# Moving the two halves of half of the weights by 64 and by 192 bytes inside their buffers

## The chip, the cores and the metric

The kernel runs on one core of a Trainium2 chip. The metric is the time of one execution on the device in microseconds (us). The kernel before takes 2594.1 us (median of three runs, 2593.63 to 2594.11).

## What is computed

The reference is a decoder trunk of two layers over 256 tokens with 2048 features, all in float32. Cut to what matters here, a layer is a row of large matrix products with small pieces of attention between them:

```python
proj = rms_norm(x, mix_norm) @ w_in              # 2048 x 6924
...
x = x + mix @ w_out                              # 2048 x 2048
x = x + cross_attention(rms_norm(x, xattn_norm), rms_norm(mem, mem_norm), wq, wk, wv, wo)
u = rms_norm(x, ffn_norm) @ ffn_w_up             # 2048 x 11264
...
x = x + (silu(gate) * val) @ ffn_w_down          # 5632 x 2048
```

The four head groups between `w_in` and `w_out` (retention, stick-breaking attention, HGRN2, sparse attention) and the cross-attention are small beside these products.

## The kernel before

**Products in three parts.** TensorE (PE in the profile) multiplies in the type float32r, which keeps fewer bits than float32. So the kernel splits each operand into a high part `hi` (the value rounded to float32r) and a low part `lo` (what is left), and adds three products: hi·hi, lo·hi and hi·lo. The activations are split when they are made, into tiles `xt` and `mg` of 128 x 2 x 256 elements: for 128 features the high parts of 256 tokens and then their low parts, 2048 bytes in each partition.

**Units of weights.** The weights come from memory in units of at most 128 x 1024 elements, 4096 bytes in each partition, in the order that `plan()` fixes. SyncE (SP) issues the transfer of a unit into a buffer `raw` (`u_dma`) six units ahead of its use. ScalarE (ACT) rounds it into `hi` (`u_hi`, L409) three units ahead, and VectorE (DVE) writes `lo` = raw - hi (`u_lo`, L415, which the profile shows at the helper's line L250) two units ahead. There are five buffers `raw`, four `hi` and three `lo`.

**Two kinds of use.** A matmul on PE has an operand that is loaded into the array first (`lhsT`, 128 columns; the profile's engine PEld shows the load) and one that is streamed through it (`rhs`, up to 512 columns). The load for the next matmul runs beside the stream of the present one.

- By feature (`group_b`): the weights are loaded and the activations are streamed. A unit gives 8 matmuls of 512 columns at L493, each with a slice of 128 columns (512 bytes) of `hi` loaded and a whole `xt` tile streamed, and then 8 matmuls of 256 columns at L496, with slices of `lo` loaded and the high half of the same `xt` tiles streamed. 448 units are used in this way, those of `ffn_w_up` among them.
- By token (`group_a`, and `group_tail` for the last of them): the activations are loaded and the weights are streamed. A unit of 1024 elements gives 12 matmuls of 512 columns at L424, L425 and L426. Some units are narrower: 396 and 384 columns for parts of `w_in`, 256 columns for the values of the cross-attention.

**Where the buffers lie.** The pool `flow` lays out `raw`, `hi`, `lo`, `xt` and `mg` one behind the other in SBUF. A first tile of 1920 bytes, named `edge` (L208), brings the first `raw` to a multiple of 2048 bytes. Buffers of 4096 and 2048 bytes follow, so each of these tiles begins at a multiple of 2048 bytes, and each slice that is loaded or streamed begins at a multiple of 512 bytes. The one exception is the second half of a unit of 396 columns, whose stream begins 1584 bytes behind the start of its buffer.

**Order of the work.** The program is written in the order of the units (the last loop of `body`): for each unit the transfer six ahead, the `hi` three ahead, the `lo` two ahead, the unit's matmuls, and a step (`tick`) of the smaller work, which lives in generators. No scheduler reorders it.

Of the kernel before, what the change touches and what calls it, by code (L numbers as in the profile page):

```python
# [9 lines left out]
F32 = mybir.dt.float32  # L10
F32R = mybir.dt.float32r
# [122 lines left out]
def shape_consts():  # L134
    f = np.float32
    i = np.arange(128)
    c = {}
    lg = np.log1p(-np.exp2(-5.0 - np.arange(H)))
    rel = (i[None, :] - i[:, None]).astype(np.float64)
    dec = np.zeros((128, H, 2, 128))  # L140
    for h in range(H):
        dec[:, h, 0] = np.where(rel >= 0, np.exp(lg[h] * np.maximum(rel, 0)), 0.0)
        dec[:, h, 1] = np.exp(lg[h] * (rel + 128))
    ident = np.eye(128)
    ones = np.ones((128, 128))
    tri = (i[:, None] >= i[None, :]) * 1.0
    M = np.zeros((128, 5, 128), np.float32)
    for n in range(128):
        M[n // 8 * 8:n + 1, 0, n] = 1
        for e, b in enumerate((8, 16, 32, 64)):  # L150
            mid = n // (2 * b) * 2 * b + b
            if n >= mid:
                M[mid - b:mid, 1 + e, n] = 1
    sbm = np.where(i[:, None] < i[None, :], 0.0, NEG)
    cm = np.concatenate([np.zeros((128, 128)), np.where(i[None, :] > i[:, None], NEG, 0.0)], axis=1)
    last = np.arange(15) * 16 + 31
    ok = np.stack([last[None, :] <= (t * 128 + i)[:, None] for t in range(2)], axis=1)
    inv = (10000.0 ** (-(np.arange(64) / 64))).astype(f)
    half_pi = np.full((128, 1), np.pi / 2)
    parts = [("ident", ident), ("ones", ones), ("inv", np.broadcast_to(inv, (128, 64))), ("hpi", half_pi),  # L160
             ("eps", np.full((128, 1), EPS)),
             ("tri", tri), ("dec", dec * SCALE), ("sbm", sbm), ("cm", cm),
             ("sel", (i[:, None] % 32 == np.arange(15)[None, :]) * 1.0), ("cadd", np.where(ok, 0.0, NEG)), ("cmul", ok * 1.0)]
    off, cols = {}, 0
    for n, a in parts:
        w = a.reshape(128, -1).shape[1]
        off[n] = (cols, w)
        cols += w
    big = np.concatenate([a.reshape(128, -1).astype(f) for _, a in parts], axis=1)
    return off, np.ascontiguousarray(big), M  # L170
# [18 lines left out]


class Unit:
    __slots__ = ("off", "cols", "nk", "pe", "end", "ks", "raw", "hi", "lo", "at")


def body(ctx, tc, w, x, xt_in, mem, mem_t, pos, consts, masks, pars, wck, wcv, fnorm, out):
    nc = tc.nc
    AHEAD, HI, LO = 6, 3, 2
    off, _, _ = shape_consts()
# [3 lines left out]
    flow = ctx.enter_context(tc.tile_pool(name="flow", bufs=1))  # L202
# [7 lines left out]
    def nm(p):  # L210
        count[0] += 1
        return f"{p}{count[0]}"
# [10 lines left out]
    def acc(shape):  # L223
        return pp.tile(shape, F32, name=nm("acc"), tag="acc", bufs=4)
# [4 lines left out]
    def f(ap):  # L229
        return ap.bitcast(F32)  # L230
# [18 lines left out]
    def tt(o, a, b, op):  # L249
        V.tensor_tensor(o, a, b, op=op)  # L250
# [102 lines left out]
    def start(gen):  # L353
        front.append(gen)
# [25 lines left out]

    units = []

    def unit(pe, end, ks):
        u = Unit()
        spec = next(units_w)
        u.off, u.nk = cursor[0], len(spec[2])
        u.cols = sum(b - a for a, b in spec[3])
        u.pe, u.end, u.ks = pe, end, ks
        u.raw = u.hi = u.lo = None
        cursor[0] += 128 * u.nk * u.cols  # L390
        units.append(u)

    def parts_of(u):

        n = u.nk * u.cols
        return ((0, n // 2), (n // 2, n)) if u.off == 0 else ((0, n),)
# [7 lines left out]

    def u_hi(u):
        n = u.nk * u.cols
        u.hi = flow.tile([128, n], F32R, name=nm("hi"), tag="hi", bufs=HI + 1, padded_shape=[128, 1024])
        for a, b in parts_of(u):
            A.copy(u.hi[:, a:b], u.raw[:, a:b])  # L409

    def u_lo(u):
        n = u.nk * u.cols
        u.lo = flow.tile([128, n], F32R, name=nm("lo"), tag="lo", bufs=LO + 1, padded_shape=[128, 1024])
        for a, b in parts_of(u):
            tt(u.lo[:, a:b], u.raw[:, a:b], f(u.hi[:, a:b]), OP.subtract)  # L415
        u.raw = None
# [11 lines left out]
    def group_a(src, klists, n, end, st=None, first=True, last=True):  # L428

        st = {} if st is None else st  # L430
        z = len(klists) - 1
        for i, kl in enumerate(klists):
            def pe(u, i=i, kl=kl):
                if first and i == 0:
                    st["ps"] = [acc([128, 512]) for _ in range(2)]
                for j, k in enumerate(kl):
                    mm_a(u, st["ps"], src(k), j, n, first and i == 0 and j == 0,
                         last and i == z and j == len(kl) - 1)

            def done():  # L440
                start(end(st.pop("ps")))
            unit(pe, done if last and i == z else None, lambda kl=kl: tuple(src(k) for k in kl))
        return st

    def group_tail(src, klists, n, end):
# [18 lines left out]
        for i, kl in enumerate(klists):  # L464
            def pe(u, i=i, kl=kl):
                if i == 0:
                    st["ps"] = [acc([128, 512]), acc([128, 512]), wk([128, 512])]
                if i < z - LO:
                    for p in range(3):
                        products(u.hi, u.lo, kl, i, p)  # L470
                elif i == z - LO:
                    late.extend((units[u.at + d].hi, units[u.at + d].lo, klists[i + d], i + d) for d in range(LO + 1))
                    for p in range(3):
                        for v in late:
                            products(*v, p)
                        end(p, st["ps"][p])
                    del late[:]
            unit(pe, None,
                 lambda i=i: tuple(src(k) for kl in (klists if i >= z - LO else klists[:i + 1]) for k in kl))
            units[-1].at = len(units) - 1  # L480

    def group_b(src, ends, order):


        sts = [{} for _ in ends]
        for g, i in order:
            def pe(u, i=i, st=sts[g]):
                if i == 0:
                    st["ps"] = [acc([128, 2, 256]) for _ in range(2)]
                xk = [src(4 * i + kk) for kk in range(4)]  # L490
                tiles = [(kk, q, kk * 256 + q * 128) for kk in range(4) for q in range(2)]
                for kk, q, at in tiles:
                    T.matmul(st["ps"][q].rearrange("p a b -> p (a b)"), lhsT=u.hi[:, at:at + 128],  # L493
                             rhs=xk[kk].rearrange("p a b -> p (a b)"), start=i == 0 and kk == 0, stop=False)
                for kk, q, at in tiles:
                    T.matmul(st["ps"][q][:, 1, :], lhsT=u.lo[:, at:at + 128], rhs=xk[kk][:, 0, :], start=False,  # L496
                             stop=i == 3 and kk == 3)

            def done(st=sts[g], end=ends[g]):
                start(end(st.pop("ps")))  # L500
            unit(pe, done if i == 3 else None, lambda i=i: tuple(src(4 * i + kk) for kk in range(4)))

    def whole(ps):

# [156 lines left out]
    def layer(l):  # L661
# [579 lines left out]
        for g, kind, segs in IN_GROUPS:  # L1241
            n = sum(SEG[s][1] - SEG[s][0] for s in segs)
            if kind == "A":
                group_a(src, pairs(range(8)), n, evs[g])
            else:
                group_b(src, [evs[g]] * 2, PAIR if g == "gq" else APART)
# [144 lines left out]

        at1 = len(units)
        group_b(lambda k: nx.k[k], [ev_xq] * 2, PAIR)
        group_b(lambda k: nm_.k[k], [ev_xk] * 2, APART)
        for v in range(2):
            group_a(lambda k: nm_.k[k], [range(4 * j, 4 * j + 4) for j in range(4)], 256, ev_xv(v))
# [163 lines left out]
    n = len(units)  # L1560
# [10 lines left out]
    first = first_norm()  # L1571
    first_parts = parts_of(units[0])
    u = units[0]
    u.hi = flow.tile([128, 1024], F32R, name=nm("hi"), tag="hi", bufs=HI + 1)
    u.lo = flow.tile([128, 1024], F32R, name=nm("lo"), tag="lo", bufs=LO + 1)
    tiles = xT.pop(0)
    for h, (a, b) in enumerate(first_parts):
        xk = [xt_tile("xt") for _ in range(2)]
# [6 lines left out]
        tt(u.lo[:, a:b], u.raw[:, a:b], f(u.hi[:, a:b]), OP.subtract)  # L1585
    u.raw = None
    u_hi(units[1])
    u_lo(units[1])
    next(first)
    u_hi(units[2])  # L1590
    next(first)
    start(first)
    for i in range(n):
# [8 lines left out]
        u = units[i]  # L1602
# [77 lines left out]
```

## Time and profile before

| | |
|---|---|
| median of three runs | 2594.1 us |
| the profiled execution: its own time | 2593.32 us |
| its span, first to last instruction | 2591.5 us |
| granted TensorE clock | 0.999 of full speed |
| PE busy | 2573.8 us, 99% of the span |
| DVE busy | 1778.5 us, 69% |
| ACT busy | 1364.5 us, 53% |

PE is busy throughout. A matmul's record in the profile is longer than the distance to the next one, because matmuls overlap; so what a matmul costs is read as the distance from its start to the start of the next, and not as its duration. The timeline merges neighbouring matmuls of one line into one row with their count, and gives starts to 0.01 us. Over a run of many matmuls the distance of one comes out to a fraction of a nanosecond.

### The profile page before, as it was taken

The numbers are of one execution on the slowest core, as the hardware profiler recorded it, in microseconds if no ns is written. First come the engines' busy times: TensorE is split into PE (matmuls) and PEld (weight loads), VectorE is DVE, ScalarE is ACT, GpSimd is POOL, SyncE is SP. The second block draws the span as 40 slices with busy tenths as digits, with TensorE's granted clock in tenths as the row PEclk, the third lists the DMA queues.
The fourth block names the chain that finished last, engine by engine and source line by source line (L and its number), as shares of the span: only waits on it lengthen the run. The fifth ranks groups of instructions, "written<-read, shape, count | busy, mean of one in ns | idle before, by whom it ended". The sixth has DMA issues, their size and how long they took to land. (4 is left out here: it accounts for less than half of the span.)

```text
span 2591.5 us, 37308 instructions
## 1 busy us (share of the span) xinstructions
PE 2573.8 (99%) x13866; PEld 2215.8 (86%) x13866; DVE 1778.5 (69%) x2881; ACT 1364.5 (53%) x2158; POOL 45.1 (2%) x79
## 2 busy tenths in 40 slices
PE   9999999999999999999999999999999999999998
PEld 7888888988888888888889888889888888888887
DVE  7776665667767676676768666656676666766766
ACT  6545545566455555454555455455654545454554
POOL 0010000000000000000000100000000000000000
PEclk9999999999999999999999999999999999999999
DMA  8574466545555555555555644655455565555664
GB/s 284 173 234 140 147 206 217 183 153 188 191 187 193 190 191 188 194 184 192 186 183 160 227 134 155 203 184 178 156 187 195 188 193 187 195 187 189 209 189 146
DMA packets 136582, 483.66 MB, mean 187 GB/s; under 512 B 15952, under 2 KB 16464, under 8 KB 136400
## 3 DMA queue, kind: packets, MB, share of 16 engines
q1 hardware_dynamic: 131024, 464.75, 54.7%
q0 software_dynamic: 4800, 15.73, 1.9%
q8 instruction: 109, 1.79, 0.3%
q10 hardware_dynamic: 576, 0.79, 0.1%
q14 instruction: 73, 0.60, 0.1%
HBM read 479.12 MB, written 2.10 MB: 186 GB/s over the span
## 5 line engine op out<-in xcount | busy, mean ns | idle before, releaser
L250 DVE TENSOR_TENSOR lo<-raw,hi 128x1024 fp32r<-128x1024 f32 (+3 forms) x881 | 1067.3, 1213 | 742.8 <-issue 264.1
L409 ACT CAST hi<-raw 128x1024 fp32r<-128x1024 f32 (+2 forms) x879 | 917.1, 1044 | 1151.0 <-PE acc L493 501.1
L493 PE MATMUL acc<-xt,hi 128*128 128x512 f32 x3456 | 870.5, 394 | 5.7 <-ACT hi L1584 5.7
L493 PEld LDWEIGHTS acc<-xt,hi 128*128 128x128 f32 x3456 | 623.7, 189 | 121.6 <-ACT hi L1584 5.7
L496 PEld LDWEIGHTS acc<-xt,lo 128*128 128x128 f32 x3456 | 472.3, 191 | 33.9
L496 PE MATMUL acc<-xt,lo 128*128 128x256 f32 x3456 | 482.6, 283 | 0.0
L424 PE MATMUL acc<-hi,mg 128*128 128x512 f32 (+1 forms) x1136 | 433.1, 381 | 0.2
L426 PE MATMUL acc<-hi,mg 128*128 128x512 f32 (+1 forms) x1136 | 428.8, 377 | 0.0
L425 PE MATMUL acc<-lo,mg 128*128 128x512 f32 (+1 forms) x1136 | 428.7, 377 | 0.0
L424 PE MATMUL acc<-hi,xt 128*128 128x512 f32 (+2 forms) x640 | 252.1, 394 | 0.0
L426 PEld LDWEIGHTS acc<-hi,mg 128*128 128x128 f32 x1136 | 213.7, 188 | 39.8 <-DVE mg L250 0.3
L424 PEld LDWEIGHTS acc<-hi,mg 128*128 128x128 f32 x1136 | 213.8, 188 | 39.3 <-ACT mg L263 1.0
L425 PEld LDWEIGHTS acc<-lo,mg 128*128 128x128 f32 x1136 | 213.9, 188 | 38.4
L426 PE MATMUL acc<-hi,xt 128*128 128x512 f32 (+2 forms) x640 | 243.2, 380 | 0.0
L425 PE MATMUL acc<-lo,xt 128*128 128x512 f32 (+2 forms) x640 | 242.8, 379 | 0.0
L253 DVE SCALAR_TENSOR_TENSOR s<-s,par,s 128x255 f32<-128x255 f32 x352 | 161.8, 480 | 6.3
L425 PEld LDWEIGHTS acc<-lo,xt 128*128 128x128 f32 x640 | 120.4, 188 | 20.8 <-issue 1.9
L424 PEld LDWEIGHTS acc<-hi,xt 128*128 128x128 f32 x640 | 120.3, 188 | 20.8 <-issue 2.3
L426 PEld LDWEIGHTS acc<-hi,xt 128*128 128x128 f32 x640 | 120.1, 188 | 20.6
L245 ACT ACTIVATE s<-s,par 128x256 f32<-128x256 f32 x176 | 96.1, 594 | 0.4 <-DVE s L250 0.4
L250 DVE TENSOR_TENSOR s<-acc,s 128x256 f32<-128x256 f32 x224 | 83.8, 416 | 0.0
L250 DVE TENSOR_TENSOR x<-x,acc 128x512 f32<-128x512 f32 x128 | 81.6, 678 | 1.5 <-PE acc L462 1.5
(202 smaller groups left out, 1421.9 us busy)
## 6 DMA issues: line engine op xcount, KB each, us to landing
raw<-in_w_dram SPq DMA_DIRECT2D x847, 512.0 KB, 3.4
raw<-in_w_dram SPq DMA_DIRECT2D x16, 396.0 KB, 3.1
raw<-in_w_dram SPq DMA_DIRECT2D x16, 384.0 KB, 3.1
s<-in_nsa_w_ck_dram POOLq DMA_DIRECT2D x16, 256.0 KB, 5.4
s<-in_nsa_w_cv_dram POOLq DMA_DIRECT2D x16, 256.0 KB, 4.8
s<-in_memt_dram POOLq DMA_DIRECT2D x16, 256.0 KB, 5.3
s<-in_xt_dram SPq DMA_DIRECT2D x8, 256.0 KB, 6.5
x<-in_x_dram SPq DMA_DIRECT2D x8, 256.0 KB, 7.1
```

What stands on the lines that cost most here:

```text
L245: A.activation(o, i, func, bias=bias, scale=scale)
L250: V.tensor_tensor(o, a, b, op=op)
L253: V.scalar_tensor_tensor(o, a, s, b, op0=op0, op1=op1)
L409: A.copy(u.hi[:, a:b], u.raw[:, a:b])
L424: T.matmul(ps[t][:, 0:n], lhsT=xh, rhs=hi, start=first, stop=False)
L425: T.matmul(ps[t][:, 0:n], lhsT=xh, rhs=lo, start=False, stop=False)
L426: T.matmul(ps[t][:, 0:n], lhsT=xl, rhs=hi, start=False, stop=last)
L493: T.matmul(st["ps"][q].rearrange("p a b -> p (a b)"), lhsT=u.hi[:, at:at + 128], rhs=xk[kk].rearrange("p a b -> p (a b)"), start=i == 0 an ...
L496: T.matmul(st["ps"][q][:, 1, :], lhsT=u.lo[:, at:at + 128], rhs=xk[kk][:, 0, :], start=False, stop=i == 3 and kk == 3)
```

## The change

The helper `unit` takes a flag `by_feature`, which `group_b` sets. The buffers `hi` and `lo` become 1088 elements (4352 bytes) instead of 1024 (4096 bytes). In a by-feature unit the low part begins 16 elements (64 bytes) behind the start of its buffer, and the high part 48 elements (192 bytes). In a by-token unit both begin at the start.

4352 is 2048 x 2 + 256. So neighbouring buffers of one kind stand 256 bytes further on, taken modulo 2048: the four `hi` buffers begin at 0, 256, 512 and 768 past a multiple of 2048, the three `lo` buffers at 0, 256 and 512. Two more filling tiles, `edge1` (1024 bytes, behind `hi`) and `edge2` (1280 bytes, behind `lo`), bring what follows back to multiples of 2048. All other tiles stand where they stood modulo 2048; they begin 4096 bytes later. By-feature slices of `hi` so begin at 192 past a multiple of 256, those of `lo` at 64 past a multiple of 256; by-token slices begin at multiples of 256.

On every engine the built program has the same instructions in the same order with the same waits. Only addresses differ.

```diff
+    def lo_tile(u):
+
+        o = flow.tile([128, 1088], F32R, name=nm("lo"), tag="lo", bufs=LO + 1)
+        at = 16 if u.by_feature else 0
+        return o[:, at:at + u.nk * u.cols]
+
+    def hi_tile(u):
+
+        o = flow.tile([128, 1088], F32R, name=nm("hi"), tag="hi", bufs=HI + 1)
+        at = 48 if u.by_feature else 0
+        return o[:, at:at + u.nk * u.cols]
...
     def u_hi(u):
         n = u.nk * u.cols
-        u.hi = flow.tile([128, n], F32R, name=nm("hi"), tag="hi", bufs=HI + 1, padded_shape=[128, 1024])
+        u.hi = hi_tile(u)
...
     def u_lo(u):
         n = u.nk * u.cols
-        u.lo = flow.tile([128, n], F32R, name=nm("lo"), tag="lo", bufs=LO + 1, padded_shape=[128, 1024])
+        u.lo = lo_tile(u)
...
-            unit(pe, done if i == 3 else None, lambda i=i: tuple(src(4 * i + kk) for kk in range(4)))
+            unit(pe, done if i == 3 else None, lambda i=i: tuple(src(4 * i + kk) for kk in range(4)), True)
...
-    u.hi = flow.tile([128, 1024], F32R, name=nm("hi"), tag="hi", bufs=HI + 1)
-    u.lo = flow.tile([128, 1024], F32R, name=nm("lo"), tag="lo", bufs=LO + 1)
+    u.hi = hi_tile(u)
+    flow.tile([128, 256], F32, name="edge1", tag="edge1")
+    u.lo = lo_tile(u)
+    flow.tile([128, 320], F32, name="edge2", tag="edge2")
```

## Rows read from the trace of the kernel before

**Rows 1.** The page's first and second part: busy time, share of the span and count of instructions of each engine, and the granted clock in 40 equal slices of the span (9 is 90% or more).

```profile
span 2591.5 us, 37308 instructions
PE 2573.8 (99%) x13866; PEld 2215.8 (86%) x13866; DVE 1778.5 (69%) x2881; ACT 1364.5 (53%) x2158; POOL 45.1 (2%) x79
PEclk9999999999999999999999999999999999999999
```

**Rows 2.** The waits of PE over the whole span: engine, tile and line that waited, whom it waited for, us in total, times, longest.

```profile
PE acc L493 <- ACT hi L1584: 5.7, 1, 5.7
PE wk L1381 <- ACT s L1370: 1.3, 2, 0.7
PE wk L1101 <- DVE s L250: 1.0, 2, 0.5
...
PE acc L461 <- DVE lo L250: 0.2, 1, 0.2
```

**Rows 3.** The groups of matmuls by line and shape: count, busy us, mean ns of one, idle before. The first two and the last are by feature, the others by token.

```profile
L493 PE MATMUL acc<-xt,hi 128*128 128x512 f32 x3456 | 870.5, 394 | 5.7 <-ACT hi L1584 5.7
L496 PE MATMUL acc<-xt,lo 128*128 128x256 f32 x3456 | 482.6, 283 | 0.0
L424 PE MATMUL acc<-hi,mg 128*128 128x512 f32 x1008 | 395.3, 392 | 0.2
...
L424 PE MATMUL acc<-hi,xt 128*128 128x512 f32 x512 | 207.6, 405 | 0.0
...
L493 PE MATMUL acc<-mg,hi 128*128 128x512 f32 x128 | 32.0, 392 | 0.0
```

**Rows 4.** The timeline of PE where by-token units (L424 to L426) give way to 32 by-feature units of `ffn_w_up` and come back: start us, us to the end of the row's last matmul, line, shape, count. Left out are 29 pairs of rows of the same kind.

```profile
850.35 0.39 PE L426 MATMUL acc<-hi,mg 128*128 128x512 f32 x1
850.58 1.98 PE L493 MATMUL acc<-xt,hi 128*128 128x512 f32 x8
852.39 1.12 PE L496 MATMUL acc<-xt,lo 128*128 128x256 f32 x8
853.35 2.00 PE L493 MATMUL acc<-xt,hi 128*128 128x512 f32 x8
855.19 1.11 PE L496 MATMUL acc<-xt,lo 128*128 128x256 f32 x8
856.14 2.00 PE L493 MATMUL acc<-xt,hi 128*128 128x512 f32 x8
...
937.14 2.00 PE L493 MATMUL acc<-xt,hi 128*128 128x512 f32 x8
938.99 1.11 PE L496 MATMUL acc<-xt,lo 128*128 128x256 f32 x8
939.94 0.40 PE L424 MATMUL acc<-hi,mg 128*128 128x512 f32 x1
```

**Rows 5.** The timeline of PE inside by-token work of 512 columns, first and last of 19 rows in a line.

```profile
276.63 0.39 PE L426 MATMUL acc<-hi,xt 128*128 128x512 f32 x1
...
280.71 0.39 PE L426 MATMUL acc<-hi,xt 128*128 128x512 f32 x1
```

**Rows 6.** The same inside by-token work of 256 columns, first and last of 27 rows in a line.

```profile
505.27 0.28 PE L426 MATMUL acc<-hi,mg 128*128 128x256 f32 x1
...
508.39 0.28 PE L425 MATMUL acc<-lo,mg 128*128 128x256 f32 x1
```

**Rows 7.** The timeline of PE after a piece of small matmuls (L1184), where by-token work of 512 columns begins again. Eleven rows in a line stand from 364.64 to 366.95.

```profile
364.33 0.48 PE L424 MATMUL acc<-hi,mg 128*128 128x512 f32 x1
364.64 0.40 PE L425 MATMUL acc<-lo,mg 128*128 128x512 f32 x1
...
366.26 0.40 PE L426 MATMUL acc<-hi,mg 128*128 128x512 f32 x1
366.50 0.39 PE L424 MATMUL acc<-hi,mg 128*128 128x512 f32 x1
...
366.95 0.39 PE L426 MATMUL acc<-hi,mg 128*128 128x512 f32 x1
```

**Rows 8.** The timeline of PE in by-token units of 396 columns: the last matmul of one unit (101.37), then a unit's six with its first half (101.55 to 102.45, streamed from the start of the buffer) and its six with the second half (102.63 to 103.53, streamed from 1584 bytes behind it).

```profile
101.37 0.34 PE L426 MATMUL acc<-hi,xt 128*128 128x396 f32 x1
101.55 0.34 PE L424 MATMUL acc<-hi,xt 128*128 128x396 f32 x1
...
102.45 0.34 PE L426 MATMUL acc<-hi,xt 128*128 128x396 f32 x1
102.63 0.34 PE L424 MATMUL acc<-hi,xt 128*128 128x396 f32 x1
...
103.53 0.34 PE L426 MATMUL acc<-hi,xt 128*128 128x396 f32 x1
```

**Rows 9.** The conversions of full weight units on DVE and ACT: count, busy us, mean ns of one, idle us before them and what ended it; and below them two of DVE's in by-feature units in the timeline, with the idle time just before.

```profile
L250 DVE TENSOR_TENSOR lo<-raw,hi 128x1024 fp32r<-128x1024 f32 x847 | 1035.2, 1223 | 730.7 <-issue 264.1 <-PE acc L425 245.8 <-PE acc L496 170.4
L409 ACT CAST hi<-raw 128x1024 fp32r<-128x1024 f32 x847 | 890.1, 1052 | 1112.8 <-PE acc L493 501.1 <-PE acc L426 459.4 <-issue 70.3
861.98 1.23 DVE L250 TENSOR_TENSOR lo<-raw,hi 128x1024 fp32r<-128x1024 f32 x1 [1.57 <-PE acc L496]
864.77 1.23 DVE L250 TENSOR_TENSOR lo<-raw,hi 128x1024 fp32r<-128x1024 f32 x1 [1.57 <-PE acc L496]
```

More of the change, by code (lines that the diff above doesn't have):

```diff
@@ L191 @@
 class Unit:
-    __slots__ = ("off", "cols", "nk", "pe", "end", "ks", "raw", "hi", "lo", "at")
+    __slots__ = ("off", "cols", "nk", "pe", "end", "ks", "raw", "hi", "lo", "at", "by_feature")
 def body(ctx, tc, w, x, xt_in, mem, mem_t, pos, consts, masks, pars, wck, wcv, fnorm, out):
@@ L381, in body, with unit @@
     units = []
-    def unit(pe, end, ks):
+    def unit(pe, end, ks, by_feature=False):
         u = Unit()
+        u.by_feature = by_feature
         spec = next(units_w)
```

## The prediction

> **What bounds the kernel now.** I read the page first. PE is busy for 2573.8 of 2591.5 us and the granted clock stands at full speed, 2.4 GHz, from end to end [rows 1]. The waits of PE come next. The longest is 5.7 us at the start, and those named after it are 1.3 us and less [rows 2]. So nothing outside PE holds it up, and the time is the sum of the distances between matmuls. What is left to read is the distance from one start to the next, in the timeline.
>
> In by-token work of 512 columns 18 distances make 280.71 - 276.63 = 4.08 us, 226.7 ns each [rows 5]. At 256 columns 26 distances make 508.39 - 505.27 = 3.12 us, 120.0 ns each [rows 6]. The difference, 106.7 ns for 256 columns, is 0.417 ns for a column, one period of 2.4 GHz. So 512 columns account for 213.3 ns, and 13.3 ns per matmul are fixed, at both widths. I call these distances the settled pace.
>
> The by-feature units don't keep that pace. Eight matmuls of 512 and eight of 256 columns would take 8 x 226.7 + 8 x 120.0 = 2773 ns. The first of the 32 units, which follows by-token work, takes 853.35 - 850.58 = 2.77 us. The next 31 take 939.94 - 853.35 = 86.59 us, 2793 ns each [rows 4]. So each unit that follows another one loses 20 ns, and the by-token work behind the last one starts slowly too. The high half of such a unit takes 855.19 - 853.35 = 1.84 us, 230 ns per matmul; that of the first unit, 852.39 - 850.58 = 1.81 us, is settled. The loss thus comes behind the switch from 256 to 512 columns.
>
> The same is seen behind small matmuls: from 364.64 to 366.95 ten by-token distances make 2.31 us, 231.0 ns each, and single ones come to 0.24 us (366.26 to 366.50), with no wait among them [rows 7]. A distance so depends on how the load of the next matmul stands against the stream of the present one, and some matmuls pass before it settles. That relation is what the change can act on.
>
> **The change part by part.** Nothing is added, removed or reordered, so there is no instruction to count. Three things move.
>
> First, the loaded slices of by-feature units: those of `hi` by 192 and those of `lo` by 64 bytes modulo 256, against streams that stay at multiples of 2048. A unit has 16 matmuls, and there are (3456 + 128) / 8 = 448 units, 7168 matmuls [rows 3]. No matmul of the trace loads float32r from such an address, so the price is bounded from both sides. Below: if the settling loss and all of the fixed 13.3 ns went, 448 x 20 ns + 7168 x 13.3 ns = 9.0 + 95.3 = 104 us less. Above: if every one of the 3584 matmuls of 512 columns took the longest distance seen, 240 ns for 230, 36 us more.
>
> Second, the streams of by-token units, which begin at multiples of 256 instead of 2048 bytes. The nearest row is that of 396 columns. There the stream begins at the buffer's start for six matmuls and 1584 bytes behind it for the next six, and the distance is 0.18 us throughout, 2.16 us for 12, with no settling at either switch [rows 8]. I cost this part at nothing. Its upper bound is the same longest distance: 3 x (1008 + 512) = 4560 matmuls of 512 columns [rows 3] x (240 - 226.7) ns = 61 us more.
>
> Third, ACT writes and DVE reads and writes at the new addresses. A `lo` conversion takes 1223 ns, a `hi` 1052 ns, and in by-feature units DVE sits idle for 1.57 us before each until PE frees a buffer [rows 9]. I cost it at nothing. PE hides it, with DVE at 1778.5 us of 2591.5 [rows 1]: over the 847 conversions each would have to grow by (2591.5 - 1778.5) / 847 = 0.96 us before DVE became the bound, and ACT's by more.
>
> The value between the bounds of the first part is a choice. The row of 396 columns is the nearest in kind, and it speaks for no effect. But there the streamed side moved and not the loaded one, and by token there is no change of width from unit to unit. The rows of the very work that is touched [rows 4] show a loss that hangs on how load and stream meet. In the new layout the loads of `lo` and of `hi` are 128 bytes apart in phase, which is 32 columns or 13.3 ns of a float32r stream, and this bears on the very switch at which the loss arises. I take it that the settling loss goes and the fixed part stays: 448 x 20 ns = 9.0 us. From the profiled execution's 2593.3 us (2591.5 of span and 1.8 around it) this gives 2584.3; the median of the runs lies 0.8 us higher, so 2585. With half of the loss left it would be 2590; with a tenth of the fixed part gone too, 9.5 us more, 2576. These are the case's own range.
>
> The Trainium skill speaks against this. On the page "SBUF — State Buffer", section "SBUF: two separate sides", it has contention on the engine side at the port pair that VectorE and GpSimd share, and says that PE never waits on anyone. By that rule no address inside SBUF matters to PE, and the time stays at 2594. The trace agrees as far as other engines go, since distances repeat while DVE and ACT come and go. It leaves open what PE's own two reads do to each other: 231 against 226.7 ns for one shape and no wait between.
>
> **The rivals.** *No effect.* The distance doesn't depend on the loaded address, and settling is a matter of the order of widths alone. For it: the flat 0.18 us at both places in the buffer [rows 8], and the settling after small matmuls by token, where all slices lie at multiples of 512, as in by-feature units [rows 4, 7]. Against it: nothing but the lack of a row with such a load. Time: 2594, give or take 4.
>
> *The fixed part falls.* If the 13.3 ns are PE's two reads meeting in the same place of SBUF, a steady offset of the loads could end that for part of the matmuls. Half of it would be 48 us, with the settling loss 57 us: 2537. For it: the fixed part is the same at 512 and 256 columns, as a cost per load would be. Against it: it is the same with slices at 0, 512, 1024 and 1536 past 2048 and with the stream moved by 1584 bytes. The Trainium skill, page "TensorE: Matmul & The Clock Gate", section "Back-to-back issue gap", gives 2.5 ns over the columns for an isolated matmul of another type. Were all of the by-feature matmuls to reach that, an estimate from this figure is 7168 x 10.8 ns = 77 us, and 2508 with the settling loss; no row here shows a float32r matmul that close to its columns.
>
> *The settled pace is lost* (slower). If offsets of 256, 512 and 768 bytes from unit to unit move the phase of load and stream each time, by-token work never settles: 4560 matmuls x (231.0 - 226.7) ns = 19.6 us, and by-feature units stay at 231 throughout, 448 x (8 x 231.0 - 1840) ns = 3.6 us. Time 2617. For it: behind a disturbance it takes some ten matmuls to settle, and a by-token unit has only twelve [rows 7]. Against it: the flat 396-column rows. It decides from a quarter of that price on, 6 us.
>
> **How the numbers follow.** No more than 0.2%, 5.2 us, can be told from no change here: below 2588.9 is faster, above 2599.3 slower. Chances: the settling loss goes 0.40 (2576 to 2590, a tenth of it above 2588.9), no effect 0.32, the fixed part falls 0.08, the settled pace is lost 0.20 (one part in twenty of it inside 0.2%). Faster: 0.36 + 0.08 = 0.44. Slower: 0.19. The same: 0.37. The likeliest case gives 2585. The range reaches from 2560, which leaves out most of the falling fixed part (0.08), to 2606, which holds the lesser half of the lost pace and leaves out 0.10. Both signs are in it; the likeliest one's own range is 2576 to 2590.
>
> **What would show it.** In the timeline of the same 32 by-feature units: 2.77 us each if the settling loss goes, 2.79 if nothing happens, under 2.72 if the fixed part falls. In by-token work 18 distances in a line should still make 4.08 us; 4.1 or more means the settled pace is lost. ACT's and DVE's mean conversion may change without any effect on the end. The forecast is wrong if units stay at 2.79 us, or if by-token rows lose what by-feature rows gain. A wait of PE for `hi` or `lo` in the middle of the span would overturn the argument that only distances count.

## The result and the profile after

The changed kernel takes 2574.9 us (median of four runs, 2574.56 to 2576.26), against 2593.9 for the kernel before on the same chip: a ratio of 0.9928, with an interval of 0.9916 to 0.9940. That is 18.9 us less, more than twice the 9.0 us of the forecast. The profiled execution took 2574.6 us, with a span of 2572.8 us.

The page of the changed kernel, its span, its busy times and the granted clock, answers to [rows 1]:

```profile
span 2572.8 us, 37308 instructions
PE 2554.7 (99%) x13866; PEld 2197.5 (85%) x13866; DVE 1777.8 (69%) x2881; ACT 1364.3 (53%) x2158; POOL 45.4 (2%) x79
PEclk9999999999999999999999999999999999999999
```

PE lost 19.1 us of busy time and the span 18.7. PE's loads (PEld) lost 18.3 with it, and no other engine changed by more than 0.7 us. PE's waits, as in [rows 2], are the old ones (engine, tile and line, whom it waited for, us in total, times, longest; the three behind these two are 1.0 us and less, as before):

```profile
PE acc L506 <- ACT hi L1599: 6.1, 1, 6.1
PE wk L1394 <- ACT s L1383: 1.3, 2, 0.7
```

The wait at the start is 0.4 us longer and nothing in the middle has appeared. So the gain, too, lies in the distances between matmuls. The groups of matmuls show in which, and below them stand the two conversions (count, busy us, mean ns, idle before; they answer to [rows 3, 9]; L493 is now L506, L496 is L509, L424 is L437):

```profile
L506 PE MATMUL acc<-xt,hi 128*128 128x512 f32 x3456 | 868.8, 394 | 6.1 <-ACT hi L1599 6.1
L509 PE MATMUL acc<-xt,lo 128*128 128x256 f32 x3456 | 465.7, 277 | 0.0
L437 PE MATMUL acc<-hi,mg 128*128 128x512 f32 x1008 | 395.3, 392 | 0.2
L437 PE MATMUL acc<-hi,xt 128*128 128x512 f32 x512 | 207.6, 405 | 0.0
L250 DVE TENSOR_TENSOR lo<-raw,hi 128x1024 fp32r<-128x1024 f32 x847 | 1034.7, 1223 | 711.5 <-issue 251.2 <-PE acc L438 245.9 <-PE acc L509 162.7
L422 ACT CAST hi<-raw 128x1024 fp32r<-128x1024 f32 x847 | 889.7, 1051 | 1094.0 <-PE acc L506 483.5 <-PE acc L439 460.6 <-issue 70.1
```

The by-feature matmuls of 256 columns (L509) went from 482.6 to 465.7 us, 16.9 of the 19.1. Those of 512 columns (L506) lost 1.7. By token nothing moved, and neither did the conversions. The records of the low parts' loads became shorter as well, from 191 to 188 ns in the mean (before, then after):

```profile
L496 PEld LDWEIGHTS acc<-xt,lo 128*128 128x128 f32 x3456 | 472.3, 191 | 33.9
L509 PEld LDWEIGHTS acc<-xt,lo 128*128 128x128 f32 x3456 | 460.0, 188 | 36.9
```

The timeline of PE over the same 32 units of `ffn_w_up` as in [rows 4] (start us, us to the end of the row's last matmul, line, shape, count):

```profile
845.84 0.39 PE L439 MATMUL acc<-hi,mg 128*128 128x512 f32 x1
846.07 2.00 PE L506 MATMUL acc<-xt,hi 128*128 128x512 f32 x8
847.91 1.08 PE L509 MATMUL acc<-xt,lo 128*128 128x256 f32 x8
848.82 2.00 PE L506 MATMUL acc<-xt,hi 128*128 128x512 f32 x8
850.66 1.07 PE L509 MATMUL acc<-xt,lo 128*128 128x256 f32 x8
851.57 2.00 PE L506 MATMUL acc<-xt,hi 128*128 128x512 f32 x8
...
933.06 1.08 PE L509 MATMUL acc<-xt,lo 128*128 128x256 f32 x8
933.97 0.40 PE L437 MATMUL acc<-hi,mg 128*128 128x512 f32 x1
```

From 848.82 to 933.97 stand 31 units: 85.15 / 31 = 2.747 us each, where before it was 2.793. The high half of a unit still takes 850.66 - 848.82 = 1.84 us, as before. The low half takes 851.57 - 850.66 = 0.91 us instead of 0.95 to 0.96. Single distances inside a typical unit, from the starts in the trace in ns:

| | eight of 512 columns | eight of 256 columns |
|---|---|---|
| before | 233 236 228 232 231 227 227 227 | 113 119, then six of 120 |
| after | 226 229 232 226 229 232 226 236 | 118 114, then six of 113.3 |

At 256 columns the settled distance fell from 120.0 to 113.3 ns. (The expectations below say 113.7: that is the whole low half, 0.91 us, over eight, with its longer first distance in it.) The columns take 106.7 ns by the prediction's working, so the part it called fixed went from 13.3 to 6.7 ns, to half. The new pace is the same from unit to unit: 382 of the 448 take 2746 or 2747 ns, though the smaller work beside them differs. At 512 columns the distances did not settle at 226.7. They became a pattern of three steps with nearly the same sum. Over all 448 by-feature units the distances from start to start add up to 428.0 us before and 410.5 after for the low halves, and 829.8 and 828.1 for the high halves: 17.5 + 1.7 us less, and with the 0.4 us of the longer first wait this is the 18.7 us of the span. By-token work adds up to 1167.3 us both times, and its settled pace is the old one of [rows 5], 18 distances in 279.96 - 275.88 = 4.08 us:

```profile
275.88 0.39 PE L439 MATMUL acc<-hi,xt 128*128 128x512 f32 x1
...
279.96 0.39 PE L439 MATMUL acc<-hi,xt 128*128 128x512 f32 x1
```

### The profile page after: what moved, and what is told of

It is laid out like the page before. It is cut to its first block, busy times and chain, and to the rows that moved or that the text cites. A ratio compares the mean times of both kernels' runs of the same rounds, so it can differ in the third digit from the quotient of the medians.

```text
span 2572.8 us, 37308 instructions
## 1 busy us (share of the span) xinstructions
PE 2554.7 (99%) x13866; PEld 2197.5 (85%) x13866; DVE 1777.8 (69%) x2881; ACT 1364.3 (53%) x2158; POOL 45.4 (2%) x79
## 5 line engine op out<-in xcount | busy, mean ns | idle before, releaser
L506 PE MATMUL acc<-xt,hi 128*128 128x512 f32 x3456 | 868.8, 394 | 6.1 <-ACT hi L1599 6.1
L506 PEld LDWEIGHTS acc<-xt,hi 128*128 128x128 f32 x3456 | 619.7, 188 | 118.1 <-ACT hi L1599 6.1
L509 PEld LDWEIGHTS acc<-xt,lo 128*128 128x128 f32 x3456 | 460.0, 188 | 36.9
L509 PE MATMUL acc<-xt,lo 128*128 128x256 f32 x3456 | 465.7, 277 | 0.0
L437 PE MATMUL acc<-hi,mg 128*128 128x512 f32 (+1 forms) x1136 | 433.2, 381 | 0.2
L437 PE MATMUL acc<-hi,xt 128*128 128x512 f32 (+2 forms) x640 | 252.1, 394 | 0.0
L437 PEld LDWEIGHTS acc<-hi,mg 128*128 128x128 f32 x1136 | 213.8, 188 | 39.4 <-ACT mg L263 1.0
L437 PEld LDWEIGHTS acc<-hi,xt 128*128 128x128 f32 x640 | 120.3, 188 | 20.9 <-issue 2.3
```

The lines of the kernel that those rows point to most:

```text
L437: T.matmul(ps[t][:, 0:n], lhsT=xh, rhs=hi, start=first, stop=False)
```

## The experiments

All edits are made to the changed kernel. Ratios are to the kernel before.

### Which of the parts brings it

Three causes were possible. Theory A: each half gains by its own offset, the low one above all. Rival B: only the 128 bytes between the two offsets count, at the switch of width. Rival C: the 256 bytes between neighbouring buffers, with no offset, do it.

**Low parts moved alone.**

```diff
     def hi_tile(u):
...
-        at = 48 if u.by_feature else 0
+        at = 0
```

> The low parts by feature stay 64 bytes behind the start of their buffer, the high parts go back to its start (modulo 256). Theory A (the cost lies in the address of each load against the stream beside it, each part for itself): the matmuls of 256 columns keep the 113.7 ns that they have in the changed kernel, which is 8 x 120.0 less 915 = about 39 to 45 ns in each of 448 units, 17 to 20 us of the 18.9; time 2574 to 2579 us. Rival B (what counts is how far the loads of the high and the low parts stand apart, and the two offsets work together only): 120.0 ns again, time 2590 to 2597. Rival C (the new stride of the buffers or the conversions make the gain): 2575, but then the kernel with the stride alone shows the same.

Measured: 2587.9 us (2587.27 to 2588.47), ratio 0.9977 (0.9967 to 0.9986), 6.0 us less. The group of low halves and the timeline of units of `ffn_w_up`:

```profile
L509 PE MATMUL acc<-xt,lo 128*128 128x256 f32 x3456 | 478.5, 281 | 0.0
```

```profile
852.68 2.00 PE L506 MATMUL acc<-xt,hi 128*128 128x512 f32 x8
854.52 1.11 PE L509 MATMUL acc<-xt,lo 128*128 128x256 f32 x8
855.46 1.32 PE L506 MATMUL acc<-xt,hi 128*128 128x512 f32 x5
```

(The view ends inside the last row, hence its five matmuls.) The low half takes 855.46 - 854.52 = 0.94 us, neither the 0.95 to 0.96 of before nor the 0.91 of the changed kernel. Its low matmuls lie at the very addresses that they have in the changed kernel, and stand 117.7 ns apart instead of 113.3. The 2587.9 us lie outside the range of every theory in the expectation.

**High parts moved alone** (the same edit in `lo_tile`).

> The high parts by feature stay 192 bytes behind the start of their buffer, the low parts go back to its start. Theory A: the matmuls of 256 columns return to 120.0 ns, and only the high half keeps its gain of 1844 - 1836 = 8 ns in a unit, 3.6 us; time 2587 to 2593 us. Rival B: 2590 to 2597, no gain at all. Rival C: 2575.

Measured: 2593.7 us, ratio 1.0 (0.999 to 1.0009). Nothing is gained on the whole. By distances from start to start the high halves add up to 827.7 us, 2.1 less than before, and the low halves to 429.8, 1.8 more: the low distances become irregular, 117 to 124 ns. The group of low halves is 1 us above that of before, 482.6 [rows 3]:

```profile
L509 PE MATMUL acc<-xt,lo 128*128 128x256 f32 x3456 | 483.6, 283 | 0.0
```

**Neither moved, only the longer buffers** (`at = 0` in both).

> The buffers of 4352 bytes and the filling tiles stay, both offsets are 0, so that all parts begin at multiples of 256 bytes. Theories A and B: units of 2.79 us as before, time 2592 to 2596 us. Rival C: 2575 us, with the units at 2.75.

Measured: 2593.6 us, ratio 0.9999 (0.9989 to 1.0008). Units take 2793 ns again, their single distances are those of before, one by one, and so is the group of low halves:

```profile
L509 PE MATMUL acc<-xt,lo 128*128 128x256 f32 x3456 | 482.4, 282 | 0.0
```

Rival C is out: the 256 bytes from buffer to buffer do nothing, by feature or by token.

So 6.0 us and 0 apart, and 18.9 together. Theory A fell, since the gains don't add up: the high parts' offset gives nothing in the sum by itself, and together with the low one it makes the low matmuls faster. Rival B fell too, since the low parts alone gained. Nor can it be another difference of the two offsets: with either part moved alone, the low parts lie 64 bytes behind the high ones modulo 256, and the two kernels differ by 5.8 us. The theory was amended: the distance depends on where the load lies against the stream, modulo some distance, *and* on the state in which the matmuls ahead left PE.

### One offset swept, the other held

In one kernel the groups of `ffn_w_up` (four units each) take offsets from 0 to 256 bytes in steps of 16, in turn; all other work stays as changed.

```diff
             elif what == "up":
+                shift[1] = 4 * (g % 17)
                 group_b(lambda q: nf.k[q], [ev_up(g)], APART[:4])
+                shift[1] = 16
```

> The units of the gated layer's first product (by feature) take their low parts at 16 x (g mod 17) bytes, g being the number of the group of four units, so that all offsets from 0 to 256 in steps of 16 stand in one trace; the high parts stay at 192. Theory A: the distance in the matmuls of 256 columns is a function of that offset, 120.0 ns at 0 and 256, 113.7 at 64, and the same in every group with the same offset; offsets that lie as far from 0 on the other side (192) may do as well. If the chip reads whole pieces of 64 bytes, it steps at multiples of 64. Rival B: the distance goes by the difference to 192, and is 120.0 at 192. Time between 2572 and 2594 us.

Measured: 2586.8 us, one run. The figures of this table and the next are medians over the units of an offset, a group's first unit left out, worked out from the starts in the trace; the medians at the offsets that are not listed lie between 2780 and 2807 ns a unit. High parts at 192:

| low parts at, bytes | unit, ns | low half, ns |
|---|---|---|
| 0 and 256 | 2787, 2786 | 938, 938 |
| 16, 32, 48 | 2780, 2767, 2787 | 948, 938, 942 |
| 64 | 2747 | 912 |
| 80, 96, 112 | 2787, 2780, 2793 | 947, 940, 956 |
| 128, 160 | 2800, 2820 | 962, 949 |
| 192, 208 | 2772, 2766 | 944, 933 |

The timeline at the change from 48 to 64 (605.47), and from 64 to 80 (616.47):

```profile
602.68 2.01 PE L508 MATMUL acc<-xt,hi 128*128 128x512 f32 x8
604.53 1.10 PE L511 MATMUL acc<-xt,lo 128*128 128x256 f32 x8
605.47 2.01 PE L508 MATMUL acc<-xt,hi 128*128 128x512 f32 x8
607.32 1.07 PE L511 MATMUL acc<-xt,lo 128*128 128x256 f32 x8
608.23 2.00 PE L508 MATMUL acc<-xt,hi 128*128 128x512 f32 x8
...
616.47 1.99 PE L508 MATMUL acc<-xt,hi 128*128 128x512 f32 x8
618.30 1.11 PE L511 MATMUL acc<-xt,lo 128*128 128x256 f32 x8
619.24 2.00 PE L508 MATMUL acc<-xt,hi 128*128 128x512 f32 x8
```

The low half goes from 0.94 to 608.23 - 607.32 = 0.91 us and back to 0.94. Sixteen bytes to either side of 64 the gain is gone. 0 and 256 read alike. Neither expectation came out whole. At 0 the low half takes 938 ns and not 8 x 120.0 = 960, and the pace changes at nearly every 16 bytes and not at multiples of 64. Nor does an offset always give one pace, as theory A had it: at 192 single units in one group run from 2741 ns, with a low half of 906, to 2784. That 2741 is the shortest unit in all the runs, but only one unit of each group has it.

The same with the high parts swept and the low ones held at 64:

```diff
+                shift[0] = 4 * (g % 17)
                 group_b(lambda q: nf.k[q], [ev_up(g)], APART[:4])
+                shift[0] = 48
```

> The mirror of the sweep of the low parts: in the gated layer's first product the high parts lie at 16 x (g mod 17) bytes, the low parts at 64 throughout. Theory A, amended after the first four runs (the pace of a matmul is a state that the loads' addresses and the matmuls ahead set together, so that an offset of one part also moves the other part's matmuls): at 0 the units take 2780 ns as with the low offset alone, at 192 2747 as in the changed kernel, and the low half changes from 117.7 to 113.7 ns with the high part's offset though its own addresses stay. Theory A as it was (each part for itself): the low half is 113.7 to 117.7 ns at all offsets of the high part alike. Units between 2740 and 2820 ns; time between 2572 and 2595 us.

Measured: 2587.9 us, one run.

| high parts at, bytes | unit, ns | low half, ns |
|---|---|---|
| 0 and 256 | 2780, 2780 | 942, 942 |
| 32 | 2820 and 2772 in turn | 944 and 917 |
| 64 | 2774 | 912 |
| 80 | 2807 | 941 |
| 96 | 2793 | 914 |
| 128 | 2780 | 922 |
| 176, 192 | 2760, 2747 | 916, 912 |
| 208 | 2797 and 2776 in turn | 942 and 914 |
| 240 | 2745 and 2782 in turn | 912 and 942 |

Where the high parts go from 80 to 96 (627.82) the low half, whose own addresses stay, goes from 627.82 - 626.88 = 0.94 to 630.61 - 629.70 = 0.91 us:

```profile
625.01 2.03 PE L508 MATMUL acc<-xt,hi 128*128 128x512 f32 x8
626.88 1.11 PE L511 MATMUL acc<-xt,lo 128*128 128x256 f32 x8
627.82 2.03 PE L508 MATMUL acc<-xt,hi 128*128 128x512 f32 x8
629.70 1.08 PE L511 MATMUL acc<-xt,lo 128*128 128x256 f32 x8
630.61 2.04 PE L508 MATMUL acc<-xt,hi 128*128 128x512 f32 x8
```

At 32, 208 and 240 the units alternate between two paces at one and the same pair of offsets, and at 48 whole groups keep either 2773 or 2800 ns. The amended theory holds: the low matmuls' pace is set by their own offset and by the work ahead of them.

### The stream moved instead of the load

By token the weights are the stream. Rival D: only the loaded side's address counts, so by-token work would not change. Here the units of `ffn_w_down` take both parts at the swept offset.

```diff
             elif what == "down":
+                shift[:] = [4 * (calls[0] % 17)] * 2
+                calls[0] += 1
```

> By feature as in the changed kernel. In the by-token units of the gated layer's second product both parts, which are streamed there, lie at 16 x (call mod 17) bytes. Theory A: loads and streams meet by their difference in address, so the by-token matmuls leave the 226.7 ns as well, at some offsets to more (up to 233) and perhaps at one to less (213 to 226); 0 and 256 alike. Rival D (only the loaded side's address counts, as the flat rows of 396 columns suggest): 226.7 ns at every offset. Time between 2570 and 2590 us.

Measured: 2584.4 us, one run. A unit of twelve matmuls takes 2720 ns at 0 and at 256, 2747 at 64, 2773 to 2812 at nearly all other offsets, and at 240 either 2720 or 2800. Twelve distances each at 0, 64 and 160 bytes in the timeline, 2.72, 2.75 and 2.81 us:

```profile
674.44 0.39 PE L439 MATMUL acc<-hi,mg 128*128 128x512 f32 x1
...
677.16 0.39 PE L439 MATMUL acc<-hi,mg 128*128 128x512 f32 x1
...
808.24 0.39 PE L439 MATMUL acc<-hi,mg 128*128 128x512 f32 x1
...
810.99 0.39 PE L439 MATMUL acc<-hi,mg 128*128 128x512 f32 x1
...
962.40 0.39 PE L439 MATMUL acc<-hi,mg 128*128 128x512 f32 x1
...
965.21 0.40 PE L439 MATMUL acc<-hi,mg 128*128 128x512 f32 x1
```

Rival D is out. At 64 by token the single distances are 226, 229, 232, the pattern of the by-feature high half at 192. With the stream at 64 and the load at 0 the load lies at -64, which is 192 modulo 256. By token at 192 they are 236 and 231 in turn, the pattern of the by-feature high half at 64 in the sweep before, and by token at 96 they are 231, 232, 237, close to the 231, 238, 231 by feature at 160. At these three places, then, what counts is the load's place less the stream's, modulo 256, and not which of the two was moved. At others the patterns don't match (by token at 16 the distances are 227 to 235, by feature at 240 mostly 226 to 229).

### Pairs of offsets

If a pair of offsets settled both halves, a unit would come to 8 x 226.7 + 8 x 113.3 = 2720 ns (2723 with the 113.7 of the expectation). Eighty pairs by feature (high parts at 0, 16, 240, 176 and 64, low parts at 0 to 240), and by token pairs of a high and a low offset:

```diff
+    pairs_tried = [(h, 4 * q) for h in (0, 4, 60, 44, 16) for q in range(16)]
...
             elif what == "up":
+                shift[:] = pairs_tried.pop(0) if pairs_tried else (48, 16)
```

> In the gated layer's first product, by feature, each group of four units takes its own pair of offsets: high parts at 0, 16, 240, 176 and 64 bytes, each with low parts at 0, 16, ... 240 bytes. Theory A as amended (the pace is a state that both parts' addresses and the matmuls ahead set): the units spread from 2740 to 2820 ns, most pairs near 2780 to 2800, and low halves under 920 ns stand with low parts at 64 and hardly elsewhere. If a pair lets the high half keep the settled 226.7 ns and the low half 113.7 ns, its units take 2723 ns, and 24 ns x 448 = 11 us more are to be had; I give that 1 in 4. A theory in which one part's offset alone sets the pace of its own half has low halves of 910 ns at 64 for every offset of the high parts.

> By feature as in the changed kernel. In the by-token units of the gated layer's second product the two parts, streamed there, lie at different offsets, one pair for each call: high parts at 0 with low parts at 16 to 240, low parts at 0 with high parts at 16 to 240, and high parts at 240 with low parts at 0 to 192 bytes. Theory A as amended: 2720 ns in a unit of 12 where both differences are 0, 2745 to 2815 at nearly all pairs, as in the sweep with equal offsets; a pair below 2720 would be a gain for both kernels, which I give 1 in 5. Rival (the loaded side's address alone counts): 2720 everywhere, which the sweep with equal offsets has spoken against.

Measured: 2590.7 and 2584.7 us, one run each. By feature no pair reaches 2723. Behind the first unit of a group, low halves under 920 ns stand in this run only with low parts at 64, and there not for every offset of the high parts: 912 with them at 64, 916 at 176, 911 or 942 in turn at 240, and 942 to 943 at 0 and 16. So the low parts' own offset alone doesn't set their pace. The best are (240, 64) with units of 2745 and 2781 in turn, (176, 64) and (0, 208) with 2760; the offsets of the change, (192, 64), stay the best steady pair at 2747. The worst is (64, 144), here one of its units of 2.82 us:

```profile
2380.18 2.02 PE L509 MATMUL acc<-xt,hi 128*128 128x512 f32 x8
...
2383.00 0.39 PE L509 MATMUL acc<-xt,hi 128*128 128x512 f32 x1
```

By token no pair is under the 2720 ns of no offset; units that don't follow small matmuls range, behind the first of a call, from 2746 to 2827. So among the pairs tried nothing more was to be gained by feature or, at 512 columns, by token. Most pairs in steps of 16 bytes were not tried.

### The work of 256 columns by token

The values of the cross-attention (`xattn_wv`, 16 units of 24 matmuls) are by token at 256 columns, and settle at 120.0 ns at 0 [rows 6]. The question was whether the sign of the difference counts: both parts at 192 (the load then lies at 64, as that of the low halves), or both at 64 (`[16, 16]` in the edit).

```diff
+        shift[:] = [48, 48]
         for v in range(2):
             group_a(lambda k: nm_.k[k], [range(4 * j, 4 * j + 4) for j in range(4)], 256, ev_xv(v))
+        shift[:] = [0, 0]
```

> The changed kernel, and in the by-token units of 256 columns (the values of the cross-attention, 16 units of 24 matmuls) both parts, streamed there, lie at 192 bytes, so that load less stream is 64 modulo 256 as in the low halves by feature. Theory A (the difference load less stream, modulo 256, counts, whichever side moves): 113.7 in place of 120.0 ns, 384 x 6.3 = 2.4 us; time 2572 to 2574 us against 2575. A theory in which only the loaded side's address counts: 120.0 ns, 2575.

> The same with 64 bytes, load less stream 192 modulo 256. Theory A: another pace than at 192 bytes, 117 to 120 ns as in the low halves by feature with the low parts at 192; time 2574 to 2576 us. If both sides of 0 are alike, 113.7 ns and 2572 to 2574.

> The changed kernel itself, on the same chip as the two variants: 2575 us, 18 to 20 us under the kernel before.

| | us, median of five (lowest to highest) | ratio (interval) |
|---|---|---|
| values at 192 | 2573.44 (2573.13 to 2574.14) | 0.9922 (0.9909 to 0.9934) |
| values at 64 | 2573.66 (2572.97 to 2573.96) | 0.9922 (0.9909 to 0.9936) |
| the changed kernel again | 2574.83 (2574.25 to 2575.41) | 0.9927 (0.9914 to 0.9939) |

Both medians are below that of the changed kernel, by 1.4 and 1.2 us. The intervals of the ratios overlap and 0.05% is below the 0.2% named in the prediction; but no run of either is as slow as the fastest of the changed kernel, and the distances of those 16 units, added up in the traces, are 1.6 and 1.4 us shorter. The expectation on the sign missed. Both kernels show two paces at one and the same offset. At 64, 24 distances behind by-feature work take 506.92 - 504.20 = 2.72 us, 113.3 ns each. Behind small matmuls 18 take 517.45 - 515.33 = 2.12 us, 117.8 each:

```profile
504.20 0.28 PE L440 MATMUL acc<-lo,mg 128*128 128x256 f32 x1
...
506.92 0.28 PE L440 MATMUL acc<-lo,mg 128*128 128x256 f32 x1
...
515.33 0.28 PE L441 MATMUL acc<-hi,mg 128*128 128x256 f32 x1
...
517.45 0.28 PE L441 MATMUL acc<-hi,mg 128*128 128x256 f32 x1
```

At 192 it is the other way round: 117.8 behind by-feature work, 113.3 behind small matmuls. Which of the two comes up is decided at the unit's beginning and kept to its end.

## Why the prediction was right and wrong

**Right: PE alone is the bound, and the gain is in distances.** No wait appeared, the conversions kept 1223 and 1051 ns, and the sum of the distances accounts for the span to 0.1 us. That it would be faster, and a time between 2560 and 2606, held as well.

**Right: multiples of 256 bytes cost by-token work nothing.** Its 18 distances still make 4.08 us, and the kernel with the longer buffers alone measured 0.9999. The rival of the lost settled pace put its price on offsets of 256, 512 and 768. There it is nothing; at other offsets it is real, mostly 2773 to 2812 for 2720 ns a unit.

**Wrong: "I take it that the settling loss goes and the fixed part stays: 448 x 20 ns = 9.0 us."** Both halves of this step failed. The high half kept its 1.84 us: the single distances changed, the loss stayed, and 1.7 us is all that it gave. The fixed part did not stay at 256 columns. It fell from 13.3 to 6.7 ns, worth 17.5 us with the first distance of each low half, which went from 113 to 118 ns. What took place is the rival called the falling fixed part, for half of the matmuls and for about half of the 13.3 ns, and not the case that was thought likeliest. The time came out near that case's range, 1 us below its end of 2576, for another reason. That it lies inside the whole range is in part luck: the range was laid to leave out most of the falling fixed part, priced at 2537, and this one stayed inside because it fell in half of the matmuls. The test named ahead, 2.77 us a unit against 2.72, could not tell the two apart at 2.747; the halves of the unit could.

**Wrong: the evidence weighed.** Against a falling fixed part the prediction held that 13.3 ns were seen with slices at 0, 512, 1024 and 1536. Modulo 256 these are one place: the sweeps read alike at 0 and 256. And for no effect it held the 396-column work, where the stream begins 1584 bytes in, which is 48 modulo 256 [rows 8]. By token at 512 columns an offset of 48 takes 2800 ns a unit for 2720. The flat row holds for its width and says nothing of another.

**Right in kind, wrong in place: the switch of width.** The prediction saw that the difference between the two offsets bears on the switch at which the loss arises. The offsets do work together, as 6.0, 0 and 18.9 us show, but what they settle is the low half behind the switch and not the high one. On the Trainium skill's page "SBUF — State Buffer", section "SBUF: two separate sides", PE never waits on anyone. The prediction read this as a rule that no address matters to PE, by which the time would have stayed at 2594, and the measured 0.9928 decides against that reading. As worded, the sentence speaks of waiting on others. No wait of PE for another engine came or went with the addresses, so no run here speaks against that; it leaves open, as the prediction said, what PE's own load and stream do to each other.

**Open.** What in the memory or in PE the load and the stream share was not seen. Offsets finer than 16 bytes were not tried, nor were the activations moved. That the pace depends on the load's place less the stream's rests on patterns found on both sides at three places, and on 0 and 256 reading alike; at other places the two sides differ, and whether that is the state that the matmuls ahead left was not tested.

## What to carry to other kernels

Where one engine is busy throughout and waits for nothing, read the distance from start to start for each kind of instruction, and don't take the smallest that the trace shows for a floor. The addresses of its operands against each other can set it: sweep them within one kernel, a group of work to each offset, and move operands together, since the gain of two offsets here was three times what they gave apart. Before an observation is used as evidence that an address doesn't matter, see whether it really differs in the part of the address that does, and in the same shape of work.

## What the runs showed that was not expected

The same float32r matmuls took 2741 to 2827 ns per by-feature unit of the sweeps by the place of their operands and of those of the matmuls ahead, 3% between the best and the worst. At one and the same addresses two steady paces exist, 113.3 and 117.8 ns at 256 columns, and which of them a unit takes depends on what ran before it.
